# Last LayerNorm 1 block set ahead of its neighbour's block sums, with three pairs' first products in front of it in place of two

## The chip, the cores and the metric

The kernel runs on one core of a Trainium2 chip. The metric is the device time of one execution in microseconds. Before the change it was 1742.12 us, the median of three runs that lie between 1740.56 and 1743.21 us.

## The reference, cut to what matters

One decoder layer for 1024 tokens and a model width of 1024. The part around the change is the end of the mixer and the start of the MLP:

```
y = concat(SSD heads, FoX heads) @ W_out
x = LayerNorm(alpha * x + (1 + gate1) * y)            # LayerNorm 1
h = x * (1 + scale2) + shift2
x = LayerNorm(alpha * x + (1 + gate2) * (relu(h W1)^2 W2))
```

All matrices are float32. The kernel multiplies each float32 product as three matmuls of rounded parts: high times high, high times low and low times high.

## The kernel before, in words

**LayerNorm 1.** The loop at L847 goes over eight blocks of 128 tokens. For each block TensorE multiplies the second half of the mixer by W_out into two PSUM banks (`out_mm`, L853). VectorE scales the result by the RMS factor and the gate (L856) and calls `norm` (L757). `norm` adds the residual (L763), gathers mean and variance (L764, L765), adds epsilon (L766), has GpSimd raise the variance to the power -0.5 (L767, the "pow"), and scales the block. For the last block the scaling is cut in two: L769 makes a bias, L770 scales the first 512 columns on VectorE, L771 the other 512 on ScalarE. For the other blocks one VectorE instruction does it (L773).

**The block sums.** The first MLP product h W1 is computed by a Strassen-like scheme with seven products on 2 x 2 blocks in place of eight. The operands on the side of h are blocks of h (`hb_hl` 1, 2, 3) and sums of them (5, 6, 4, 7). `to_h2` (L801) makes them for one token block: eight transposes on TensorE into two PSUM tiles (L809), eight activations on ScalarE that apply scale2 and shift2 and write the tiles `h2_t` (L816; two buffers, of the tag `o_half`), the split of the lower blocks into high and low part (L823), and for token blocks 4 to 7 four differences (L827 to L830, which the profile shows at the helper's line L791). These four run on GpSimd, but for blocks 6 and 7 on VectorE. `to_h2` of a block is called one block late: block 6's behind block 7's `norm`, block 7's at L1020, behind the first products.

**The pairs.** Sixteen pairs of column blocks of W1 follow (`Pair`, L933). A pair does the products 1, 2, 5, 6, 4, 7, 3. `w1_ops` (L886) loads its weights and gives the operands one by one: those of products 1 and 2 are plain quarters, while for product 5 and the rest four GpSimd sums of 128 x 512 come first (L923 to L926). Each operand is split by ScalarE (high, L81) and VectorE (low, L85) into a `w_op` tile. Products 1 and 2 need only `hb_hl` 1 and 2, which are made from token blocks 0 to 3. So pairs 0 and 1 do products 1 and 2 (48 matmuls of 128 x 512) ahead of the last `to_h2`. Then four `h_split` calls (L1024 to L1027) split the sums of all eight blocks into `h2_s` tiles, of which product 5 needs those of L1024 first.

**PSUM.** There are eight banks: one of the tag `mm`, two of `t`, one of `o`, and two tiles of two banks each of the tag `S`. Pairs 0 and 1 hold mm, o and t, t for products 1 and 2, and take one S tile each later. From pair 2 on a pair holds either mm, o, t, t or both S tiles. The transposes of `to_h2` and the small RMS sums (L621) use S tiles as well.

**The order of the work.** The program is written in one order, and when it is built a planner puts every engine's instructions in a fixed queue, by the times of its own simulation and with preference for what is written earlier. `after(ins)` (L70) makes everything that the block issues on the engine of `ins` come behind `ins` in that engine's queue. On the chip each queue then runs strictly in order. All DMAs are issued from SP's queue.

Of the kernel before, what the change touches and what calls it, by code (L numbers as in the profile page):

```python
# [11 lines left out]
AF = mybir.ActivationFunctionType  # L12
ALU = mybir.AluOpType
# [3 lines left out]
P = 128  # L17
# [3 lines left out]
TB = T // P  # L21
# [11 lines left out]
def layer_kernel(ctx, tc, x, xT, cols, rows3, w_ada, b_ada, w_in, w_dtf, w_out, ln_rows, w1, w2, out):  # L33
    nc = tc.nc
# [15 lines left out]
    def T4(tag, name, dt=F32, shape=(P, 1024)):  # L50
        return sb.tile(list(shape), dt, name=name, tag=tag, bufs=SLOTS[tag])
# [6 lines left out]
    def PT(tag, name, shape=(P, 512), dt=F32):  # L58
        return ps.tile(list(shape), dt, name=name, tag=tag, bufs=PB[tag])
# [9 lines left out]
    @contextmanager  # L69
    def after(ins):  # L70

        with tc.issue_after(ins.ins):
            yield

    def split(raw, hi, lo, hi_eng="pool", scale=None, lo_eng="dve"):

        if scale is None:
            if hi_eng == "pool":
                nc.gpsimd.tensor_scalar(hi, raw, 1.0, 1.0, op0=ALU.mult, op1=ALU.mult)  # L79
            elif hi_eng == "act":  # L80
                nc.scalar.copy(hi, raw)  # L81
            else:
                nc.vector.tensor_copy(hi, raw)
            eng = nc.vector if lo_eng == "dve" else nc.gpsimd
            eng.tensor_tensor(lo, raw, hi.bitcast(F32), op=ALU.subtract)  # L85
        else:
            nc.scalar.activation(hi, raw, AF.Copy, scale=scale)
            nc.vector.scalar_tensor_tensor(lo, raw, scale, hi.bitcast(F32), op0=ALU.mult, op1=ALU.subtract)
# [17 lines left out]
    mhalf = cst.tile([P, 8], F32, name="mhalf")  # L106
# [31 lines left out]
    marks = {}  # L138
# [27 lines left out]
    NP = NF // 2  # L166
# [65 lines left out]
    def proj(w, half, M=P, o=None, tag="mm", ks=range(KT)):  # L232
        if o is None:
            o = PT(tag, "mm_ps")
        ts = slice(half * 512, half * 512 + 512)
        for k in ks:
            whi, wlo = wk_(w, k)
            mm(o[:M], whi, hT[k][0][:, ts], k == 0, False)
            mm(o[:M], whi, hT[k][1][:, ts], False, False)
            mm(o[:M], wlo, hT[k][0][:, ts], False, k == KT - 1)  # L240
        return o
# [18 lines left out]
    for half in range(2):  # L260
        o = proj([dtf_t[:, :, 0:4, :], dtf_t[:, :, 4:8, :]], half, 32, tag=("mm", "o")[half])
        nc.vector.tensor_copy(dtf_raw[:32, half * 512:half * 512 + 512], o[:32])
    tp = PT("t", "t_ps", (P, 8, 32))
# [7 lines left out]
    u, s_, s2, q_ = (wk[:, i, :] for i in range(4))  # L271
# [485 lines left out]
    def norm(u, o, last):  # L757

        st = sm.tile([P, 2, 6], F32, name="bn", tag="bn", bufs=2)
        mv = sm.tile([P, 4], F32, name="mv", tag="mv", bufs=2)  # L760
        for i in range(2):
            ds = slice(i * 512, i * 512 + 512)
            nc.vector.tensor_tensor(u[:, ds], o[i], u[:, ds], op=ALU.add)  # L763
            nc.vector.bn_stats(st[:, i, :], u[:, ds])  # L764
        nc.vector.bn_aggr(mv[:, 0:2], st)  # L765
        nc.vector.tensor_scalar(mv[:, 2:3], mv[:, 1:2], LN_EPS, None, op0=ALU.add)  # L766
        nc.gpsimd.tensor_tensor(mv[:, 3:4], mv[:, 2:3], mhalf[:, 0:1], op=ALU.pow)  # L767
        if last:
            nc.vector.scalar_tensor_tensor(mv[:, 2:3], mv[:, 0:1], -1.0, mv[:, 3:4], op0=ALU.mult, op1=ALU.mult)  # L769
            nc.vector.tensor_scalar(u[:, :512], u[:, :512], mv[:, 0:1], mv[:, 3:4], op0=ALU.subtract, op1=ALU.mult)  # L770
            nc.scalar.activation(u[:, 512:], u[:, 512:], AF.Identity, bias=mv[:, 2:3], scale=mv[:, 3:4])  # L771
        else:
            nc.vector.tensor_scalar(u, u, mv[:, 0:1], mv[:, 3:4], op0=ALU.subtract, op1=ALU.mult)  # L773

# [15 lines left out]
    def sub(eng, o, a, b):  # L790
        eng.tensor_tensor(o, a, b, op=ALU.subtract)  # L791
# [9 lines left out]
    def to_h2(tb, u):  # L801
        js = slice(tb % 4 * P, (tb % 4 + 1) * P)
        eng = nc.vector if tb >= TB - 2 else nc.gpsimd
        hts = []
        for hb in range(2):
            tp = PT("S", "t_ps")
            for b in range(4):
                k = hb * 4 + b
                nc.tensor.transpose(tp[:, b * P:(b + 1) * P], u[:, k * P:(k + 1) * P], identf)  # L809
            if tb < 4:  # L810
                ht = hf[hb][:, :, js]
            else:
                ht = sm.tile([P, 4, P], F32, name="h2_t", tag="o_half", bufs=2)
            for b in range(4):
                k = hb * 4 + b
                nc.scalar.activation(ht[:, b, :], tp[:, b * P:(b + 1) * P], AF.Identity, bias=b2t[:, k:k + 1],  # L816
                                     scale=g2t[:, k:k + 1])
            hts.append(ht)
            o = (1, 2)[hb] if tb < 4 else (None, 3)[hb]
            if o:  # L820
                for i in range(2):
                    t = hb_hl[o][i]
                    split(ht[:, 2 * i:2 * i + 2, :], t[:, :, 0, js], t[:, :, 1, js], "act")  # L823
        if tb >= 4:
            b12, b22 = hts
            t1, t4 = hf[0][:, :, js], hf[1][:, :, js]
            sub(eng, t1, b12, t1)  # L827
            sub(eng, t3f[:, :, js], b22, b12)
            sub(eng, t2f[:, :, js], b22, t1)
            sub(eng, t4, t4, t2f[:, :, js])  # L830
        store(x2d[tb], u)

    def u_pre(tb):

        u = T4("misc", "u1")
        load(u, u0d[tb])
        xt = T4("raw", "x_t")
        load(xt, x[tb * P:(tb + 1) * P, :])
        nc.gpsimd.tensor_tensor(u, u, g1row, op=ALU.mult)
        nc.vector.scalar_tensor_tensor(u, xt, ALPHA, u, op0=ALU.mult, op1=ALU.add)  # L840
        return u
# [3 lines left out]
    before = None  # L845
    u = u_pre(0)
    for tb in range(TB):  # L847
        ynext = y_block(1, tb + 1, "cum") if tb + 1 < TB else None
        os_ = []
        for half in range(2):  # L850
            ds = slice(half * 512, half * 512 + 512)
            o = PT(("mm", "o", "t", "t")[(2 * tb + half) % 4], "mm_ps")
            out_mm(o, y, wo, half, range(KT))  # L853
            if half == 1 and ynext is not None:
                y_rms(ynext)
            nc.vector.scalar_tensor_tensor(o, o, y[1], g1row[:, ds], op0=ALU.mult, op1=ALU.mult)  # L856
            os_.append(o)
        norm(u, os_, last=tb == TB - 1)
        if before is not None:
            to_h2(*before)  # L860
        before = (tb, u)
        y = ynext
        if tb + 1 < TB:
            u = u_pre(tb + 1)
# [68 lines left out]
    class Pair:  # L933
        def __init__(self, n):
            self.n = n
            self.w = w1_ops(n)
            self.ready = []
            if n < 2:
                zv = None
                self.bank = {b: PT(t, "f_ps") for b, t in zip("XY", (("mm", "o"), ("t", "t"))[n])}  # L940
            elif n % 2 == (n < 7):
                xy, zv = PT("S", "f_ps", (P, 1024)), PT("S", "f_ps", (P, 1024))
                self.bank = {"X": xy[:, :512], "Y": xy[:, 512:], "Z": zv[:, :512], "V": zv[:, 512:]}
            else:
                self.bank = {b: PT(t, "f_ps") for b, t in zip("XYZV", ("mm", "o", "t", "t"))}
            self.e = T4("ex", "f_e", shape=(P, 4, 512))
            self.c = HX("a_c")
            self.s = None
# [63 lines left out]
            store(ad[5:7, :, at, :].rearrange("o p c -> p o c"), t)  # L1012

    ORDER = (1, 2, 5, 6, 4, 7, 3)
    first = [Pair(0), Pair(1)]
    for p in first:
        p.run(ORDER[:2])
    for p in first:
        p.ready.append(next(p.w))
    to_h2(*before)  # L1020
    for p in first:
        zv = PT("S", "f_ps", (P, 1024))
        p.bank.update(Z=zv[:, :512], V=zv[:, 512:])
    h_split(5, lambda k: hf[0][:, k, :], ["qk"] * 4)  # L1024
    h_split(6, lambda k: t2f[:, k, :], ["qk"] * 4)
    h_split(4, lambda k: hf[1][:, k, :], ["v", "v", "w", "w"])
    h_split(7, lambda k: t3f[:, k, :], ["pt"] * 4)  # L1027
    for p in first:
        p.run(ORDER[2:])
    for n in range(2, NP):  # L1030
        Pair(n).run(ORDER if n < NP - 1 else (5, 4, 1, 6, 7, 2, 3))


# [64 lines left out]
    X = [xb[j // 2][:, j % 2 * 512:j % 2 * 512 + 512] for j in range(4)]  # L1098
    product(1, X, True, False)
    take(11, X)  # L1100
    Y = [PT(t, "y_ps") for t in ("mm", "o", "t", "t")]
# [10 lines left out]
    for tb in range(TB):  # L1112
        x2 = T4("misc", "x2")
        load(x2, x2d[tb])
        for h in range(2):
            ds = slice(h * 512, h * 512 + 512)
            o = RES[(11, 12, 21, 22)[tb // 4 * 2 + h]][:, tb % 4, :]
# [4 lines left out]
    Y = [PT(t, "y_ps") for t in ("mm", "o", "t", "t")]  # L1122
# [42 lines left out]
    for tb in range(TB):  # L1165
# [4 lines left out]
        for half in range(2):  # L1170
            ds = slice(half * 512, half * 512 + 512)
# [4 lines left out]
        mv = norm2(us, oh)  # L1176
        if not last:
            nc.vector.scalar_tensor_tensor(mv[:, 2:3], mv[:, 0:1], -1.0, mv[:, 3:4], op0=ALU.mult, op1=ALU.mult)
        for h, u in enumerate(us):
            ds = slice(h * 512, h * 512 + 512)  # L1180
# [66 lines left out]
```

## Time and profile before

| | before |
|---|---|
| median of three runs | 1742.12 us |
| range of the runs | 1740.56 to 1743.21 us |
| profiled execution | 1744.44 us, its span 1742.7 us |
| TensorE busy | 1654.0 us, 95% of the span |
| VectorE busy | 1229.9 us, 71% |
| GpSimd busy | 821.6 us, 47% |
| ScalarE busy | 747.2 us, 43% |
| mean granted TensorE clock | 0.98 |

TensorE is busy nearly all the time, so time is to be found where it stops. The lists of instructions in order of time show for each piece its start, its length, its engine and line, and in brackets how long the engine had been idle and what ended that. The pieces of one engine can overlap a little, since the next starts while the one before drains. PEclk is the granted clock of TensorE as a share of full speed.

### The profile page before, as it was taken

What the parts mean: (1) busy time and instruction counts of PE and PEld (TensorE: products, weight loads), DVE (VectorE), ACT (ScalarE), POOL (GpSimd) and SP (SyncE); (2) the same over time, 40 slices, a digit from 0 to 9 for tenths busy, and PEclk for the clock granted to TensorE, in tenths of its full rate; (3) what the DMA queues carried; (4) which work ended last, traced back from release to release, by engine and by line L of the source; (5) the groups of instructions that cost most, each with busy time, mean ns of one, the idle gap of its engine ahead of it and who ended that gap; (6) DMA issues with size and microseconds to landing.
All of it is one profiled execution on the core that took longest, in us unless ns stands there. A gap on an engine that the chain in (4) does not pass through costs nothing.

```text
span 1742.7 us, 22932 instructions
## 1 busy us (share of the span) xinstructions
PE 1654.0 (95%) x8316; PEld 1368.7 (79%) x8316; DVE 1229.9 (71%) x1898; ACT 747.2 (43%) x1321; POOL 821.6 (47%) x670
## 2 busy tenths in 40 slices
PE   8989899899999999999899999799999999999996
PEld 6777787788877878888778887688888878888885
DVE  7755777686777777676665379986767855646668
ACT  3458355414444444444565334633332334343322
POOL 5121332256566466454442345566656624704535
PEclk9999999999999999999999999899999999999998
DMA  8134343334444534434324644043444596676512
GB/s 331 37 123 147 109 145 109 121 130 151 161 142 170 169 134 167 137 121 132 119 97 130 221 157 169 37 175 133 146 143 160 172 340 212 247 242 205 194 36 96
DMA packets 112032, 268.72 MB, mean 154 GB/s; under 512 B 10128, under 2 KB 37008, under 8 KB 111920
## 3 DMA queue, kind: packets, MB, share of 16 engines
q1 hardware_dynamic: 111920, 267.27, 44.2%
q8 instruction: 65, 1.06, 0.3%
q14 instruction: 47, 0.39, 0.1%
HBM read 194.22 MB, written 64.62 MB: 149 GB/s over the span
## 4 chain that ended last, share of the span: by engine, by line
PE 60%; DVE 15%; DMA 8%; ACT 7%; POOL 5%; issue 4%; SPq 0%; DVEq 0%; ACTq 0%; POOLq 0%
PE mm_ps L62 18%; PE f_ps L957 15%; PE s_ps L1073 9%; PE y_ps L1073 7%; PE s_ps L62 5%; PE o_ps L62 4%; DVE ada_red L134 3%; PE t_ps L546 3%; DMA w_b<-in_w_dram 2%; ACT scores L417 2%; POOL w_b L182 2%; DMA raw_ada<-in_w_ada_dram 1%; DVE w_hl L85 1%; DVE conv_a L346 1%; DVE h_hl L85 1%
## 5 line engine op out<-in xcount | busy, mean ns | idle before, releaser
L62 PE MATMUL mm_ps<-h_hl,w_hl 128*128 128x512 f32 x2016 | 504.5, 400 | 10.9 <-POOL w_hl L79 6.1
L62 PEld LDWEIGHTS mm_ps<-h_hl,w_hl 128*128 128x128 f32 x2016 | 373.5, 191 | 88.3 <-POOL w_hl L79 6.9
L85 DVE TENSOR_TENSOR w_op<-raw_w,w_op 128x512 fp32r<-128x512 f32 (+1 forms) x149 | 186.9, 1260 | 23.2 <-ACT w_op L81 22.6
L957 PE MATMUL f_ps<-h_s,w_op 128*128 128x512 f32 x768 | 183.8, 394 | 6.4 <-ACT h_s L81 3.3
L957 PEld LDWEIGHTS f_ps<-h_s,w_op 128*128 128x128 f32 x768 | 146.0, 190 | 38.4 <-ACT h_s L81 3.7
L524 POOL TENSOR_SCALAR probs<-probs,m 128x128 f32<-128x128 f32 (+7 forms) x128 | 104.5, 822 | 127.3 <-DVE m L523 122.8
L81 ACT CAST w_op<-raw_w 128x512 fp32r<-128x512 f32 (+1 forms) x149 | 114.5, 774 | 100.2 <-PE f_ps L957 53.0
L1073 PE MATMUL s_ps<-w_op,a_op 128*128 128x512 f32 x672 | 153.7, 390 | 1.5 <-DVE a_op L85 1.1
L1073 PEld LDWEIGHTS s_ps<-w_op,a_op 128*128 128x128 f32 x672 | 125.9, 188 | 28.8 <-DVE a_op L85 1.6
L79 POOL TENSOR_SCALAR w_hl<-raw_w 128x512 fp32r<-128x512 f32 x86 | 60.5, 705 | 180.0 <-PE mm_ps L62 126.1
L85 DVE TENSOR_TENSOR a_op<-a_ld,a_op 128x1024 fp32r<-128x1024 f32 x53 | 75.5, 1427 | 98.4 <-ACT a_op L81 98.4
L132 POOL TENSOR_TENSOR raw_ada<-raw_ada,c_act 128x1024 f32<-128x1024 f32 x44 | 88.8, 2027 | 117.1 <-DMA raw_ada<-in_w_ada_dram 99.8
L522 ACT ACTIVATE probs<-probs,m 128x128 f32<-128x128 f32 (+7 forms) x128 | 99.1, 775 | 96.8 <-DVE m L521 86.5
L957 PE MATMUL f_ps<-h_hl,w_op 128*128 128x512 f32 x576 | 136.9, 389 | 0.0
L85 DVE TENSOR_TENSOR w_hl<-raw_w,w_hl 128x512 fp32r<-128x512 f32 x88 | 81.5, 929 | 68.5 <-POOL w_hl L79 68.2
L548 ACT CAST pt_hl<-t_ps 128x512 fp32r<-128x512 f32 (+1 forms) x160 | 84.8, 542 | 100.7 <-PE t_ps L546 97.3
L957 PEld LDWEIGHTS f_ps<-h_hl,w_op 128*128 128x128 f32 x576 | 108.0, 188 | 22.4
L81 ACT CAST a_op<-a_ld 128x1024 fp32r<-128x1024 f32 x53 | 55.7, 1054 | 159.7 <-PE s_ps L1073 80.7
L62 PE MATMUL o_ps<-pt_hl,v_s 128*128 128x256 f32 (+1 forms) x640 | 110.9, 300 | 8.7 <-DVE pt_hl L549 5.4
L549 DVE TENSOR_TENSOR pt_hl<-t_ps,pt_hl 128x512 fp32r<-128x512 f32 (+1 forms) x160 | 99.6, 630 | 23.1 <-ACT pt_hl L548 21.6
L519 DVE CUSTOM_DVE_ANT_0 probs<-s_ps,cumrow 128x128 f32<-128x128 f32 (+7 forms) x128 | 94.8, 750 | 28.9 <-PE s_ps L62 20.1
L1073 PE MATMUL y_ps<-w_op,a_op 128*128 128x512 f32 x504 | 114.7, 389 | 0.0
(254 smaller groups left out, 3136.1 us busy)
## 6 DMA issues: line engine op xcount, KB each, us to landing
raw_w<-in_w_dram SPq DMA_DIRECT2D x57, 512.0 KB, 4.3
a_ld<-ad SPq DMA_DIRECT2D x49, 512.0 KB, 4.4
raw_ada<-in_w_ada_dram SPq DMA_DIRECT2D x48, 512.0 KB, 3.6
raw_w<-in_w_in_dram SPq DMA_DIRECT2D x44, 512.0 KB, 3.7
w_b<-in_w_dram SPq DMA_DIRECT2D x14, 1024.0 KB, 8.0
w2t<-w_b SPq DMA_DIRECT2D x14, 1024.0 KB, 4.3
ad<-a_s SPq DMA_DIRECT2D x28, 512.0 KB, 3.4
raw_w<-w2t SPq DMA_DIRECT2D x28, 512.0 KB, 4.8
```

What stands on the lines that cost most here:

```text
L62: nc.tensor.matmul(o, l, r, start=start, stop=stop)
L79: nc.gpsimd.tensor_scalar(hi, raw, 1.0, 1.0, op0=ALU.mult, op1=ALU.mult)
L81: nc.scalar.copy(hi, raw)
L85: eng.tensor_tensor(lo, raw, hi.bitcast(F32), op=ALU.subtract)
L132: nc.gpsimd.tensor_tensor(raw, raw, c_act.unsqueeze(2).broadcast_to([P, KT, P]), op=ALU.mult)
L519: nc.vector.tensor_tensor_reduce(out=pt, in0=sp[:, :W], in1=cum[:, :W], op0=ALU.add, op1=ALU.max, scale=1.0, scalar=-3.0e38, accum_out=m[: ...
L522: nc.scalar.activation(pt, pt, AF.Exp, bias=m[:, 1:2], scale=1.0, accum_out=m[:, 2:3])
L524: nc.gpsimd.tensor_scalar(pt, pt, m[:, 3:4], 1.0, op0=ALU.mult, op1=ALU.mult)
L548: nc.scalar.copy(hl[:, 0, :n], tp[:, :n])
L549: nc.vector.tensor_tensor(hl[:, 1, :n], tp[:, :n], hl[:, 0, :n].bitcast(F32), op=ALU.subtract)
L957: nc.tensor.matmul(o, l, r, start=first and k == 0 and m == 0, stop=last and k == 3 and m == 2, skip_group_check=True)
L1073: nc.tensor.matmul(banks[j], ahl[a_][:, n, js], whl[w_][:, n, :], start=first and d == 0 and n == 0 and m == 0, stop=last and d == ND - 1 ...
```

## The change

For the last block the bias and the ScalarE half are gone, and VectorE scales both halves; the pow and the second half are kept as marks. Block 6's `to_h2` is put behind the second half: this binds what it issues on VectorE. The transposes of a block share one PSUM tile of two banks. Three pairs do their products 1 and 2 ahead of the last `to_h2`; the third operand of pairs 0 and 1, with its GpSimd sums, is put behind the pow and behind the scaling. Pair 2 holds one S tile for its first products, pair 1 takes o and t for its other two banks, and the later pairs take both S tiles when their number is even.

```diff
@@ norm
-        nc.gpsimd.tensor_tensor(mv[:, 3:4], mv[:, 2:3], mhalf[:, 0:1], op=ALU.pow)
+        marks["pow"] = nc.gpsimd.tensor_tensor(mv[:, 3:4], mv[:, 2:3], mhalf[:, 0:1], op=ALU.pow)
         if last:
-            nc.vector.scalar_tensor_tensor(mv[:, 2:3], mv[:, 0:1], -1.0, mv[:, 3:4], op0=ALU.mult, op1=ALU.mult)
-            nc.vector.tensor_scalar(u[:, :512], u[:, :512], mv[:, 0:1], mv[:, 3:4], op0=ALU.subtract, op1=ALU.mult)
-            nc.scalar.activation(u[:, 512:], u[:, 512:], AF.Identity, bias=mv[:, 2:3], scale=mv[:, 3:4])
+            for i in range(2):
+                ds = slice(i * 512, i * 512 + 512)
+                marks["ln"] = nc.vector.tensor_scalar(u[:, ds], u[:, ds], mv[:, 0:1], mv[:, 3:4], op0=ALU.subtract,
+                                                      op1=ALU.mult)
@@ to_h2
+        tps = PT("S", "t_ps", (P, 1024))
         for hb in range(2):
-            tp = PT("S", "t_ps")
+            tp = tps[:, hb * 512:hb * 512 + 512]
@@ loop over blocks
-        if before is not None:
+        if before is not None and tb == TB - 1:
+
+            with after(marks["ln"]):
+                to_h2(*before)
+        elif before is not None:
             to_h2(*before)
@@ Pair.__init__
-            elif n % 2 == (n < 7):
+            elif n == 2:
+                xy = PT("S", "f_ps", (P, 1024))
+                self.bank = {"X": xy[:, :512], "Y": xy[:, 512:]}
+            elif n % 2 == 0:
@@ first pairs
-    first = [Pair(0), Pair(1)]
+    first = [Pair(n) for n in range(3)]
     for p in first:
         p.run(ORDER[:2])
-    for p in first:
-        p.ready.append(next(p.w))
+    with after(marks["ln"]), after(marks["pow"]):
+        for p in first[:2]:
+            p.ready.append(next(p.w))
     to_h2(*before)
-    for p in first:
-        zv = PT("S", "f_ps", (P, 1024))
-        p.bank.update(Z=zv[:, :512], V=zv[:, 512:])
...
     for p in first:
+        if p.n == 1:
+            p.bank.update(Z=PT("o", "f_ps"), V=PT("t", "f_ps"))
+        else:
+            zv = PT("S", "f_ps", (P, 1024))
+            p.bank.update(Z=zv[:, :512], V=zv[:, 512:])
         p.run(ORDER[2:])
-    for n in range(2, NP):
+    for n in range(3, NP):
```

## Rows read from the trace of the kernel before

**Rows 1.** The busy time of each engine over the whole span, in us, as a share of the span, and the number of instructions.
```profile
PE 1654.0 (95%) x8316; PEld 1368.7 (79%) x8316; DVE 1229.9 (71%) x1898; ACT 747.2 (43%) x1321; POOL 821.6 (47%) x670
```

**Rows 2.** Busy time by stretch around the end of LayerNorm 1. The columns are the stretch, its length, the busy time and the number of instructions of each engine, the granted TensorE clock, the DMA share and GB/s. The last row is a stretch of the pairs well behind the change.
```profile
1100.00:1110.00 10.00, 6.03 (x27) 4.67 (x25) 9.96 (x14) 1.55 (x3) 8.69 (x7) 1.00 0.00 0
1110.00:1120.00 10.00, 4.19 (x13) 2.92 (x14) 8.85 (x13) 10.00 (x24) 2.99 (x2) 0.52 0.14 55
1120.00:1130.00 10.00, 10.00 (x37) 8.01 (x37) 10.00 (x18) 7.56 (x16) 0.64 (x1) 0.79 0.00 0
...
1140.00:1160.00 20.00, 20.00 (x90) 16.57 (x89) 17.20 (x17) 7.33 (x13) 16.74 (x11) 1.00 0.51 186
```

**Rows 3.** TensorE in order of time, from the first products of the pairs on: start, length, engine, line, tiles, count, and the idle time before with what ended it.
```profile
1094.86 11.17 PE L957 MATMUL f_ps<-h_hl,w_op 128*128 128x512 f32 x48
1110.16 1.68 PE L809 MATMUL t_ps<-identf,u 128*128 128x128 f32 x8 [4.13 <-DVE u L770]
1115.09 1.22 PE L957 MATMUL f_ps<-h_s,w_op 128*128 128x512 f32 x2 [3.25 <-ACT h_s L81]
1118.71 21.42 PE L957 MATMUL f_ps<-h_s,w_op 128*128 128x512 f32 x82 [2.40 <-DVE h_s L85]
```

**Rows 4.** The same columns as in Rows 2, for single microseconds in which the granted clock falls and rises.
```profile
1110.00:1111.00 1.00, 0.84 (x6) 0.87 (x7) 1.00 (x3) 1.00 (x3) 0.00 (x0) 0.73 0.00 0
...
1123.00:1124.00 1.00, 1.00 (x4) 0.72 (x4) 1.00 (x3) 0.82 (x3) 0.00 (x0) 0.50 0.00 0
1124.00:1125.00 1.00, 1.00 (x6) 0.82 (x5) 1.00 (x3) 0.42 (x1) 0.00 (x0) 0.95 0.00 0
```

**Rows 5.** Pieces of the chain of work that ended last: start, length, and engine, tile and line. The last is its first long piece on TensorE behind the change.
```profile
1108.42 1.15 DVE mv L769
1109.59 0.81 ACT u L771
...
1118.71 61.31 PE f_ps L957 x258
```

**Rows 6.** VectorE in order of time, with the columns of Rows 3, from block 6's scaling to the low parts of the first sums.
```profile
1091.50 1.77 DVE L773 TENSOR_SCALAR u<-u,mv 128x1024 f32<-128x1024 f32 x1 [0.67 <-POOL mv L767]
...
1094.58 2.80 DVE L85 TENSOR_TENSOR h_hl<-h_t,h_hl 128x256 fp32r<-128x256 f32 x2
...
1097.91 1.17 DVE L85 TENSOR_TENSOR w_op<-raw_w,w_op 128x512 fp32r<-128x512 f32 x1
1099.00 0.75 DVE L856 SCALAR_TENSOR_TENSOR mm_ps<-mm_ps,r_rms,g1row 128x512 f32<-128x512 f32 x1
1099.67 1.12 DVE L85 TENSOR_TENSOR w_op<-raw_w,w_op 128x512 fp32r<-128x512 f32 x1
1100.70 0.68 DVE L763 TENSOR_TENSOR u<-mm_ps,u 128x512 f32<-128x512 f32 x1
1101.42 0.69 DVE L764 BATCH_NORM_STATS2 bn<-u 128x6 f32<-128x512 f32 x1
1102.03 1.70 DVE L791 TENSOR_TENSOR h_f<-h_t,h_f 128x512 f32<-128x512 f32 x1
...
1103.77 1.65 DVE L791 TENSOR_TENSOR h_t<-h_t 128x512 f32<-128x512 f32 x1
1105.34 0.14 DVE L766 TENSOR_SCALAR mv<-mv 128x1 f32<-128x1 f32 x1
1105.40 0.68 DVE L791 TENSOR_TENSOR h_t<-h_t,h_f 128x512 f32<-128x512 f32 x1
1106.00 0.75 DVE L85 TENSOR_TENSOR h_hl<-h_t,h_hl 128x256 fp32r<-128x256 f32 x2
1106.67 1.75 DVE L791 TENSOR_TENSOR h_f<-h_f,h_t 128x512 f32<-128x512 f32 x1
1108.34 1.21 DVE L769 SCALAR_TENSOR_TENSOR mv<-mv 128x1 f32<-128x1 f32 x1
1109.48 0.54 DVE L770 TENSOR_SCALAR u<-u,mv 128x512 f32<-128x512 f32 x1
...
1112.87 0.69 DVE L791 TENSOR_TENSOR h_f<-h_t,h_f 128x512 f32<-128x512 f32 x1 [0.45 <-ACT h_t L816]
1114.26 0.69 DVE L791 TENSOR_TENSOR h_t<-h_t 128x512 f32<-128x512 f32 x1 [0.70 <-ACT h_t L816]
...
1115.47 1.50 DVE L85 TENSOR_TENSOR h_hl<-h_t,h_hl 128x256 fp32r<-128x256 f32 x1
```

**Rows 7.** GpSimd in order of time, with the same columns: a sum of a pair's weights, the last block's pow, the last sums of pair 1, and the next sum.
```profile
1091.43 1.29 POOL L791 TENSOR_TENSOR w_s<-raw_w 128x512 f32<-128x512 f32 x1
...
1105.56 0.93 POOL L767 TENSOR_TENSOR mv<-mv,mhalf 128x1 f32<-128x1 f32 x1 [0.69 <-ACT w_op L81]
1106.46 3.08 POOL L791 TENSOR_TENSOR raw_w<-raw_w 128x512 f32<-128x512 f32 x2
1115.03 1.66 POOL L791 TENSOR_TENSOR w_s<-raw_w 128x512 f32<-128x512 f32 x1 [5.50 <-DVE h_t L791]
```

**Rows 8.** SP's queue in order of time: the last early load of weights, and the stores of blocks 6 and 7.
```profile
1089.11 0.33 SPq L65 DMA_DIRECT2D raw_w<-in_w_dram  x1
1093.30 17.45 SPq L65 DMA_DIRECT2D x2d<-u  x2
```

**Rows 9.** Who TensorE waited for between 1000 and 1125 us: in total, how often, the longest.
```profile
PE t_ps L809 <- DVE r_rms L624: 2.3, 2, 1.2
```

## The prediction

> **What bounds the kernel now.** I read the engine shares first: TensorE is busy 95% of the span, VectorE 71% [rows 1]. So time can only be won where TensorE stops or runs slowly, and the table of stretches shows such a place at the seam between LayerNorm 1 and the pairs: 6.03 us busy out of ten from 1100 us, 4.19 from 1110, and a granted clock of 0.52 and 0.79 in the two stretches from 1110 and from 1120 [rows 2]. TensorE's own order of time says what it lacks there. After 48 early matmuls it stops 4.13 us until block 7's scaling (L770) lets the transposes start, then 3.25 us for the high and 2.40 us for the low parts of the first sums [rows 3]. That is 9.8 us, and with the clock falling from full (2.4 GHz) to half (1.2 GHz) at about 1110.7 us and rising at about 1124, it works at half rate from 1118.7 to 1124, which costs another 2.7 us [rows 3, 4].
>
> The chain of waits says who is late: it leaves VectorE only for ScalarE pieces near 1110 and joins TensorE at 1118.71 [rows 5]. VectorE was busy 9.96 us out of ten from 1100 [rows 2]. In its queue, block 6's four differences (1.70, 1.65, 0.68, 1.75 us) and two low splits (0.75 together) stand ahead of or between the last steps of block 7's norm, and L769 takes 1.21 us for a 128 x 1 result [rows 6]. The reader should see two prices for the same kind of instruction: a 128 x 512 difference is 0.68 us where GpSimd is idle (1105.40) and 1.7 us where GpSimd runs its own sums. The instructions that read PSUM (0.69 and 0.75) or do statistics (0.69) keep their price [rows 6, 7].
>
> **The change, part by part.** The profiled execution took 1744.44 us with a span of 1742.7; the median of the runs is 1742.12, 2.3 lower. I work out a difference on this trace and take it off the median. About 0.2% (3.5 us) is what a measurement can tell from no change.
>
> *Pair 2's first two products.* 24 matmuls move into the hole. Well behind the seam 90 take 20 us, 0.222 each [rows 2], so later work shrinks by 5.3 us. At the early rate, 48 in 11.17 us or 0.233 each [rows 3], 72 end at 1094.86 + 16.8 = 1111.6. This is the gain of the whole change: as TensorE has the transposes behind these products, it can't profit from anything earlier.
>
> *The transposes.* They start at about 1111.6 in place of 1110.16 [rows 3], 1.4 us later, if block 7 is scaled by then. Were they put between the pairs, the delay would be 0.
>
> *Block 7's norm.* From 1094.58 to the end of L770 at 1110.02 VectorE spends 15.4 us. Block 6's work, 6.5 us, and L769, 1.2 us, leave it. The second half adds 0.54, and the wait for the pow, filled by block 6 before, is now bare: 0.67 as it was for block 6 [rows 6]. Pair 2's first split takes the place of one of pair 0's, which moves behind the norm. That gives 1103.5. GpSimd's weight sums, which began at 1091.43, now start behind the pow, so the stretch in front of it is quieter: of the two low splits at 2.80 one at 0.4 and one at 1.5 remain, and two weight splits fall from 1.17 and 1.12 to 0.68 [rows 6, 7], 1.8 us less. Block 7 is scaled by 1101.7, ten microseconds ahead of TensorE.
>
> *VectorE until block 7's first difference* (1112.87 before, after 0.45 us of idle time). It does the same work in another order plus two splits for pair 2: one quiet (0.68), one beside GpSimd (1.12), together +1.8. The second half against L769 is -0.7, the bare wait +0.7, the quiet stretch -1.8. GpSimd's eight sums now all run from the pow on, beside block 6's work. I price it that the one difference that ran alone goes from 0.68 to 1.75 and one low split from 0.4 to 1.5 [rows 6], +2.2. Sum +2.2, less the two idle waits of 0.45 and 0.70 that it fills: +1.0. Bounds: both splits quiet and no clash added, -1.5; every clash, see the second rival.
>
> *What sets the resumption.* VectorE asks for +1.0, TensorE's transposes for +1.4; the later counts. So the sums and with them the work of 1118.71 come 1.4 us later, with 5.3 us less to do: a gain of **3.9 us**. Between no delay and the VectorE bound of the second rival it is 5.3 to 1.3.
>
> *The clock.* TensorE now works at full speed until 1111.6 and then waits once for the sums, still some 5 to 7 us with little in between. I take the half-rate stretch as it was, worth nothing; the bound is the 2.7 us that it costs now.
>
> *Edits taken at nothing.* The moved sums of pairs 0 and 1 are eight of 1.3 to 1.6 us [rows 7], about 12 us from the pow at 1101: pair 0's second is done by 1104, pair 1's second by 1110, ahead of the resumption. If GpSimd were late, each would cost TensorE its own 1.5 us. GpSimd's next sum waited 5.50 us for block 7's differences before [rows 7] and still does. ScalarE gives up L771 (0.81 us on the chain, rows 5), and its part is priced above. SP's queue holds block 7's store until L771's half is done, 17.45 us in one piece [rows 8]; it comes free earlier, and pair 2's last early load was issued at 1089.11 ahead of it, so nothing is late. Sharing one PSUM tile for the eight transposes takes away two waits for the RMS sums, 2.3 us together [rows 9]; at that time VectorE is what TensorE's results wait for, so I give it 0, up to 2.3. The later pairs' banks: pair 1's o and t come free with its first products' results, and even pairs still alternate with odd ones. Should one be late, TensorE waits for one PSUM read of 0.7 us.
>
> **The rivals.** *The clock stays up.* One wait in place of two may not bring it down. For it: until 1111.6 TensorE has no hole left. Against it: the 4.13 us stop was followed by the fall [rows 3, 4], and the remaining wait is as long. Then 2.7 us more are won: 3.9 + 2.7 = 6.6, 1735.5 us.
>
> *VectorE and GpSimd block each other all the way.* From 1101.7 nine two-input instructions (block 6's six, three weight splits) meet eight GpSimd sums. At 1.75 us for eight and 0.68 for the last, VectorE reaches block 7's first difference at 1116.4, not at 1112.42 when it came free before: 4.0 us later, a gain of 1.3, 1740.8 us. For it: three of block 6's four differences had this price [rows 6]. Against it: the fourth and the two low splits at 1106.00 hardly had, with GpSimd busy for half the time. The Trainium skill, page "SBUF — State Buffer", section "Who interferes with whom", says that a VectorE instruction with two SBUF inputs and a GpSimd instruction that reads SBUF exclude each other for the whole instruction; by that rule it would be this case. The trace agrees as far as it goes: 1.7 against 0.68.
>
> *Pair 2's second operand comes late (slower).* Its place is VectorE's queue. Its `w_op` tile needs a buffer that pair 0's first product frees at 1094.86 + 2.8 = 1097.7. If the planner therefore sets its low split behind block 6's six instructions, it ends at 1101.7 + 7 x 1.75 = 1114.0. TensorE has run out after 60 matmuls at 1108.8 and stands 5.1 us, with block 7's transposes queued behind the 12 that are left: 1116.8 against 1110.16, 6.6 us late. A stop of that length is followed by the half clock, as the 4.13 us one was, and the 12 cost 2.8 us more. Sum 5.3 - 6.6 - 2.8 = -4.1: 1746.2 us. It decides from a split that ends after 1108.8 and loses from about 1112.7 on. For it: the norm alone is pinned ahead of block 6, not the split. Against it: written earlier, it is preferred, and ScalarE had little to do before 1105.
>
> *The change does not do what it says*, since the scaling ends no earlier: TensorE is then covered until 1111.6 all the same and block 6's 6.5 us fall behind 1110. That is the second rival's time, and part of its chance.
>
> **How the numbers follow.** The forecast 60%: 1742.12 - 3.9 = 1738.2 us; with its own bounds (gain 1.3 to 5.3, and up to 1.5 more where upstream waits give something back) it lies above 3.5 us in 41 of the 60. Clock stays up 10%, faster. Mutual blocking 16%: 14 same, 2 slower. Late operand 14%: 10 slower, 4 same where the split is less late. Faster 0.51, same 0.37, slower 0.12. The range reaches from 1733.5 (clock up, and 2 us of the bounds) to 1743.5, past the second rival and short of the full price of the third.
>
> **What would show it.** In the changed profile: 72 early matmuls without a gap from about 1095 to 1111.6; block 7's scaling near 1102 with block 6's differences behind it; transposes right behind the 72 with no wait for L770's successor; the next matmul on sums at about 1120, a wait of some 7 us in all, and the half clock to about 1125; no new wait for PSUM banks in the pairs. It is wrong if TensorE stops after 48 or 60 matmuls, if the resumption lies beyond 1122, or if the clock holds at 1.00.

## The result, and the profile after

The change made the kernel slower: 1755.31 us (median of six runs, 1754.55 to 1757.95) against 1741.36 us for the kernel before in the same session (six runs, 1740.03 to 1743.21), a ratio of 1.0082 with an interval of 1.0069 to 1.0095. The profiled execution took 1756.47 us with a span of 1754.7, 12.0 us more than before. TensorE's busy time hardly moved (1652.4 us against 1654.0 in [rows 1]), so the time was lost in stops.

TensorE of the kernel after in order of time, with the columns of [rows 3]. It stands against those rows:

```profile
1087.39 6.88 PE L966 MATMUL f_ps<-h_hl,w_op 128*128 128x512 f32 x29
1094.11 0.60 PE L811 MATMUL t_ps<-identf,u 128*128 128x128 f32 x4
1094.46 7.33 PE L966 MATMUL f_ps<-h_hl,w_op 128*128 128x512 f32 x31
1101.63 0.60 PE L811 MATMUL t_ps<-identf,u 128*128 128x128 f32 x4
1107.20 1.11 PE L811 MATMUL t_ps<-identf,u 128*128 128x128 f32 x4 [4.97 <-ACT h_t L818]
1111.12 0.80 PE L966 MATMUL f_ps<-h_s,w_op 128*128 128x512 f32 x1 [2.81 <-ACT h_s L81]
1112.28 4.28 PE L966 MATMUL f_ps<-h_s,w_op 128*128 128x512 f32 x11 [0.36 <-DVE h_s L85]
1129.98 17.17 PE L966 MATMUL f_ps<-h_s,w_op 128*128 128x512 f32 x62 [13.42 <-ACT f_e L979]
```

Sixty matmuls (29 + 31) stand ahead of block 7's transposes, not 72. The second half of these transposes waits 4.97 us, until ScalarE has read the first half, which lies in the same tile. Then product 5 of pair 0 runs (1 + 11 matmuls), and TensorE stops for **13.42 us**: product 6 adds to the bank that ScalarE's copy of product 1 (L979) has to read first. What ScalarE does until then, in order of time:

```profile
1104.08 1.66 ACT L81 CAST w_op<-raw_w 128x512 fp32r<-128x512 f32 x3 [3.86 <-POOL raw_w L789]
1105.65 1.50 ACT L818 ACTIVATE h_t<-t_ps,b2t,g2t 128x128 f32<-128x128 f32 x4
...
1117.32 2.17 ACT L81 CAST h_s<-h_f 128x512 fp32r<-128x512 f32 x4
1119.39 0.61 ACT L81 CAST w_op<-w_s 128x512 fp32r<-128x512 f32 x1
1128.30 0.62 ACT L81 CAST w_op<-raw_w 128x512 fp32r<-128x512 f32 x1 [8.30 <-POOL raw_w L792]
1128.83 0.61 ACT L81 CAST w_op<-w_s 128x512 fp32r<-128x512 f32 x1
1129.35 0.58 ACT L979 COPY f_e<-f_ps 128x512 f32<-128x512 f32 x1
```

The copy needs nothing that is late. Two casts stand ahead of it in the queue. The first, of `raw_w`, is pair 2's operand of product 3, which comes from the last of GpSimd's four sums for pair 2. No product needs this operand for a long time yet. GpSimd's queue shows why the sums are late (these rows stand against [rows 7]), and VectorE's what runs meanwhile:

```profile
1111.10 13.15 POOL L792 TENSOR_TENSOR w_s<-raw_w 128x512 f32<-128x512 f32 x1 [3.97 <-DVE h_t L792]
1124.33 1.26 POOL L789 TENSOR_TENSOR raw_w<-raw_w 128x512 f32<-128x512 f32 x1
1125.67 2.60 POOL L792 TENSOR_TENSOR raw_w<-raw_w 128x512 f32<-128x512 f32 x2
```

```profile
1094.90 2.94 DVE L771 TENSOR_SCALAR u<-u,mv 128x512 f32<-128x512 f32 x2 [0.45 <-POOL mv L767]
...
1109.74 0.68 DVE L792 TENSOR_TENSOR h_f<-h_t,h_f 128x512 f32<-128x512 f32 x1
1110.34 0.68 DVE L792 TENSOR_TENSOR h_t<-h_t 128x512 f32<-128x512 f32 x1
...
1115.23 4.89 DVE L85 TENSOR_TENSOR h_s<-h_t,h_s 128x512 fp32r<-128x512 f32 x8
1120.04 2.48 DVE L85 TENSOR_TENSOR h_s<-h_f,h_s 128x512 fp32r<-128x512 f32 x4
1122.45 0.68 DVE L85 TENSOR_TENSOR w_op<-w_s,w_op 128x512 fp32r<-128x512 f32 x1
1128.95 0.69 DVE L85 TENSOR_TENSOR w_op<-raw_w,w_op 128x512 fp32r<-128x512 f32 x1 [5.82 <-ACT w_op L81]
```

One sum of the kind that took 1.66 us before [rows 7] takes 13.15 us. It lasts through an unbroken row of VectorE instructions with two SBUF inputs, and ends 1.1 us after the last of them (1122.45 + 0.68 = 1123.13, against 1111.10 + 13.15 = 1124.25).

The first two lines of ScalarE show the same pattern on a smaller scale. Block 7's first transposes are done at 1102.23, but ScalarE reads them only from 1105.65 on, behind three casts of weights, for the first of which it waited 3.86 us on a GpSimd sum that the change had moved. That makes TensorE's 4.97 us so long. It costs nothing that can be seen, since VectorE has no pause before block 7's first difference at 1109.74.

Of the waits of TensorE from 980 us to the end, with the columns of [rows 9], those on r_rms shown there are gone, and those on VectorE's low parts of the weights (L85) are 3.6 us (0.8 before):

```profile
PE f_ps L966 <- DVE w_op L85: 3.6, 4, 1.4
```

Busy time by stretch, with the columns of [rows 2]:

```profile
1100.00:1110.00 10.00, 3.34 (x16) 2.34 (x15) 10.00 (x10) 4.79 (x12) 6.97 (x5) 0.76 0.00 1
1110.00:1120.00 10.00, 5.08 (x12) 3.37 (x12) 10.00 (x18) 9.55 (x19) 8.90 (x1) 0.67 0.00 0
1120.00:1130.00 10.00, 0.02 (x1) 0.02 (x1) 4.18 (x8) 1.70 (x5) 8.04 (x4) 0.50 0.00 0
1130.00:1140.00 10.00, 10.00 (x32) 8.05 (x33) 4.82 (x8) 3.25 (x6) 0.00 (x0) 0.70 0.00 0
```

**The account of the profiled executions.** The first early matmul starts 7.5 us sooner (1087.39 against 1094.86). Of this, 3.7 us were there already at the last step of L659, in work that the change does not touch; 3.8 us come from the rest of the LayerNorm 1 stage. From that matmul to the first one of the second stage it is 339.2 us against 321.3, 17.9 us more: the stop 13.4; waits on `w_op` 3.6 - 0.8 = 2.8; half clock after the stops, 9.2 us of work at it against 5.4, half of the difference, 1.9; the sums 24.9 us behind the first early matmul against 23.9, 1.0; less 12 x 0.222 = 2.7 for what moved ahead. That is 16.4; 1.5 us of the 17.9 stay unassigned. In the second stage 1.6 us more go with a dip of the clock (0.66 from 1429 to 1434 us). The sum, 17.9 + 1.6 - 7.5, is the 12.0 of the spans.

### The profile page after: what moved, and what is told of

It reads as the page before. It is cut to its first block, busy times and chain, and to the rows that moved or that the text cites. A ratio compares the mean times of both kernels' runs of the same rounds, so it can differ in the third digit from the quotient of the medians.

```text
span 1754.7 us, 22925 instructions
## 1 busy us (share of the span) xinstructions
PE 1652.4 (94%) x8316; PEld 1364.6 (78%) x8316; DVE 1234.9 (70%) x1898; ACT 746.5 (43%) x1320; POOL 829.7 (47%) x670
## 5 line engine op out<-in xcount | busy, mean ns | idle before, releaser
L85 DVE TENSOR_TENSOR w_op<-raw_w,w_op 128x512 fp32r<-128x512 f32 (+1 forms) x149 | 193.2, 1303 | 34.7 <-ACT w_op L81 34.2
L966 PE MATMUL f_ps<-h_s,w_op 128*128 128x512 f32 x768 | 185.6, 397 | 17.4 <-ACT f_e L979 13.4
L85 DVE TENSOR_TENSOR a_op<-a_ld,a_op 128x1024 fp32r<-128x1024 f32 x53 | 76.8, 1450 | 99.1 <-ACT a_op L81 99.0
L85 DVE TENSOR_TENSOR w_hl<-raw_w,w_hl 128x512 fp32r<-128x512 f32 x88 | 79.5, 906 | 66.1 <-POOL w_hl L79 65.9
L62 PE MATMUL o_ps<-pt_hl,v_s 128*128 128x256 f32 (+1 forms) x640 | 106.5, 290 | 8.5 <-DVE pt_hl L549 4.6
```

Source lines behind the costliest of these rows:

```text
L62: nc.tensor.matmul(o, l, r, start=start, stop=stop)
L966: nc.tensor.matmul(o, l, r, start=first and k == 0 and m == 0, stop=last and k == 3 and m == 2, skip_group_check=True)
```

## The experiments

Before's median lies between 1741.4 and 1742.5 us in all sessions. "Stop" is TensorE's wait for pair 0's copies, "sum" the first GpSimd sum of pair 2; both are read from the one profiled execution of each kernel.

| kernel | transposes' PSUM | block 7 first | pairs ahead | pair 2's cast | median us | sum us | stop us |
|---|---|---|---|---|---|---|---|
| before | two tiles | no | 2 | | 1742.5 | 1.66 | none |
| shared transposes only | one tile | no | 2 | | 1737.84 | 13.19 | 0.57 |
| LayerNorm first only | two tiles | yes | 2 | | 1743.98 | 13.18 | 0.96 |
| both of these | one tile | yes | 2 | | 1740.85 | 13.17 | 1.78 |
| three pairs, old norm, cast moved | one tile | no | 3 | behind | 1744.67 | 13.78 | 4.05 |
| three pairs, old norm | one tile | no | 3 | ahead | 1753.12 | 13.15 | 12.64 |
| after, cast moved | one tile | yes | 3 | behind | 1745.97 | 13.78 | 3.71 |
| after | one tile | yes | 3 | ahead | 1755.31 | 13.15 | 13.42 |

### The cast behind the copies

```diff
-                    nc.scalar.copy(p1, bank["X"])
+                    marks["p1", self.n] = nc.scalar.copy(p1, bank["X"])
...
-        p.run(ORDER[2:])
+        if p.n == 2:
+            with after(marks["p1", 1]):
+                p.run(ORDER[2:])
+        else:
+            p.run(ORDER[2:])
```

> The changed kernel, with one instruction of ScalarE's queue moved: pair 2's first cast that needs GpSimd's sums (the operand of product 3) comes behind the copies of pairs 0 and 1 out of PSUM in place of two places ahead of pair 0's. Theory A (a queue made the stop: the cast waits for GpSimd's sums of pair 2, which VectorE's unbroken run of splits holds up, and pair 0's copy stands behind the cast): the stop of 13.4 us falls to about 4, what is left being the splits and casts that the copy has to wait for in any case; about 9.5 us faster than the changed kernel, some 1745 us, while GpSimd's sum still takes over 10 us. Theory B (the PSUM plan: with three pairs nothing else is left for TensorE): the stop stays above 10 us, 1753 to 1757 us. Theory C (VectorE itself is slowed by GpSimd): no change either, and the first sums' splits no shorter.

Measured: 1745.97 us, ratio to before 1.0025 (1.0013 to 1.0037). In the queues two instructions have changed places: this cast, four places further back in ScalarE's (behind the other cast and three copies), and its low part, two places further back in VectorE's. ScalarE and GpSimd of this run:

```profile
1118.54 1.13 ACT L81 CAST w_op<-w_s 128x512 fp32r<-128x512 f32 x2
1119.57 0.57 ACT L979 COPY f_e<-f_ps 128x512 f32<-128x512 f32 x1
...
1128.16 0.62 ACT L81 CAST w_op<-raw_w 128x512 fp32r<-128x512 f32 x1 [7.06 <-POOL raw_w L792]
```

```profile
1110.24 13.78 POOL L792 TENSOR_TENSOR w_s<-raw_w 128x512 f32<-128x512 f32 x1 [3.97 <-DVE h_t L792]
```

The sum is as slow as before the edit; the cast waits for it as long; but the copy no longer does. The stop falls from 13.42 to 3.71 us, 9.7 us, and the median by 9.3, as theory A expected. So two thirds of the loss are the place of one cast in ScalarE's queue, together with a GpSimd sum that is held.

### LayerNorm first alone, and three pairs without it

Of the change, the first kernel keeps only the new order of norm and the third operands of pairs 0 and 1 behind it, with two pairs. The second is the kernel after with the old norm, scaled by VectorE and ScalarE behind block 6's sums; these lines of its edit leave the pinning out:

```diff
-    with after(marks["ln"]), after(marks["pow"]):
-        for p in first[:2]:
-            p.ready.append(next(p.w))
+    for p in first[:2]:
+        p.ready.append(next(p.w))
```

> The kernel before with only the reordering of the norm: block 7's scaling on VectorE alone and ahead of block 6's sums, the third operands of pairs 0 and 1 behind it; two early pairs, transposes in two PSUM tiles. By the prediction's sum the stop of 4.13 us before the transposes goes, and VectorE's work up to block 7's first difference is about the same: 0 to 3 us faster than the kernel before, 1738 to 1741.5 us. Theory A: no stop for a copy, since no pair 2 is in the queues yet. Rival (the reordering by itself starves GpSimd): a new stop of 5 us or more here too, 1746 us or more.

> The changed kernel with the norm's old order: three early pairs and the new PSUM plan, but block 7's scaling in two halves on VectorE and ScalarE behind block 6's sums, and nothing pinned. ScalarE's queue again has pair 2's cast ahead of pair 0's copy, and GpSimd's sums of pair 2 behind block 7's differences. Theory A: a stop of about 10 to 14 us as in the changed kernel, 1752 to 1757 us. Rival (the reordered norm made the stop): no stop above 5 us, 1737 to 1742 us.

Measured: 1743.98 us, ratio 1.0012 (1.0000 to 1.0025), and 1753.12 us, 1.0064 (1.0042 to 1.0086). LayerNorm first gains nothing and misses its forecast of 0 to 3 us. The transposes no longer wait for block 7's scaling, and the stop comes one step later, as this run of TensorE shows:

```profile
1091.94 11.14 PE L962 MATMUL f_ps<-h_hl,w_op 128*128 128x512 f32 x48
1102.93 1.03 PE L810 MATMUL t_ps<-identf,u 128*128 128x128 f32 x8
1114.71 1.22 PE L962 MATMUL f_ps<-h_s,w_op 128*128 128x512 f32 x2 [10.75 <-ACT h_s L81]
```

Before it was 4.13 + 3.25 + 2.40 = 9.78 us [rows 3], here 10.75 + 0.27. VectorE has to get through the same differences first. Most of the loss is there without LayerNorm first (ratio 1.0064, against 1.0082 for the whole change), with a stop of 12.64 us.

### VectorE's row broken

The kernel after; the low parts of the sums 6, 4 and 7 are left out and filled with zeros, so that each of VectorE's twelve splits with two inputs becomes two zero fills, which are set behind the splits of L1024.

```diff
-            split(src(k), t[:, 0, :], t[:, 1, :], "act")
...
+                nc.scalar.copy(t[:, 0, :], src(k))
+                with after(marks["h5"]):
+                    for _ in range(2):
+                        nc.vector.memset(t[:, 1, :].bitcast(F32), 0.0)
```

> The changed kernel with VectorE's twelve low splits of the sums for products 6, 4 and 7 replaced by two fills with zero each (the low parts of these sums are left out), which read nothing. If VectorE's instructions with two inputs hold up GpSimd, pair 2's first sum takes under 4 us in place of 13.15; if that sum is slow for a reason of its own, it stays above 8 us. The planner puts pair 0's copy ahead of the cast here, so the total is not comparable; by theory A it lies near 1743 us.

Measured, one run: 1745.92 us. GpSimd's sum:

```profile
1113.18 4.69 POOL L792 TENSOR_TENSOR w_s<-raw_w 128x512 f32<-128x512 f32 x1 [3.97 <-DVE h_t L792]
```

4.69 us in place of 13.15: it ends 1.2 us after VectorE's last two-input instruction ahead of the fills (1115.43 + 1.28 = 1116.71), while the fills go on. So the row of two-input instructions is what holds it, though the figure is above the 4 us expected. The total says less, since the planner put the copy ahead of the cast here too.

### The shared transpose tile alone, and with each of the other parts

```diff
+        tps = PT("S", "t_ps", (P, 1024))
         for hb in range(2):
-            tp = PT("S", "t_ps")
+            tp = tps[:, hb * 512:hb * 512 + 512]
```

> The kernel before with one part of the change alone: the two transpose tiles of a block are the halves of one tile of two PSUM banks. If the 3.8 us that the LayerNorm 1 stage became shorter after the change come from this part (TensorE no longer waits there for the r_rms tiles), this kernel is 2 to 4 us faster than before: 1738 to 1740 us, with the first W_f product some 3.8 us sooner after the last load-side step of ScalarE than before (94.9 against 98.7 us). Rival: the second half of a block's transposes must then wait for the reading of the first half (4.97 us for block 7 after the change), and eats the gain: 1742 to 1745 us.

> The kernel before with two parts of the change, the shared transpose tile and block 7's LayerNorm first, two pairs ahead as before. The shared tile alone gave 1737.84 us, LayerNorm first alone gave nothing (1743.98). Theory: VectorE's work sets when the W_f sums go on, so LayerNorm first gives nothing here either: 1736 to 1740 us. Rival: LayerNorm first costs time by itself, because its steps stand ahead of work that the sums need: 1741 to 1745 us.

> The kernel after without block 7's LayerNorm first, and with ScalarE's cast put behind the copies: third pair and shared transpose tile alone. With the shared tile alone (1737.84), the shared tile and LayerNorm first, and the whole change with the cast moved (1745.97) it makes a square. Theory: the third pair costs the 6 to 8 us between 1738 and 1746 whichever way LayerNorm stands, since VectorE, which sets when the sums go on, has pair 2's splits ahead of them: 1742 to 1746 us, with a stop behind pair 0's copy of 3 to 5 us. Rival: the third pair is harmless once the cast is moved, and LayerNorm first is what costs: 1736 to 1740 us.

Measured: 1737.84 us, ratio 0.9975 (0.9964 to 0.9985); 1740.85, 0.9993 (0.9979 to 1.0008), between the two ranges that were expected; 1744.67, 1.0013 (1.0000 to 1.0026). This part alone has **the lowest median of the study** and is faster than before and after; the kernel before with one-bank tiles (1738.36, below) can't be told from it. TensorE with the shared tile alone:

```profile
1101.37 0.60 PE L810 MATMUL t_ps<-identf,u 128*128 128x128 f32 x4
1105.40 0.65 PE L810 MATMUL t_ps<-identf,u 128*128 128x128 f32 x4 [3.43 <-ACT h_t L817]
1109.98 8.85 PE L958 MATMUL f_ps<-h_s,w_op 128*128 128x512 f32 x24 [3.93 <-ACT h_s L81]
1119.40 13.89 PE L958 MATMUL f_ps<-h_s,w_op 128*128 128x512 f32 x60 [0.57 <-ACT f_e L971]
```

The RMS waits of 2.3 us [rows 9] are gone, and the seam costs 3.43 + 3.93 = 7.4 us in place of 9.8: 4.7 us together, as much as the median fell. (The two profiled executions differ by 8.0 us, so this is a sum of the main waits and no full account.) GpSimd's sum is held in this run too (13.19 us) and costs nothing, since no cast that needs it stands ahead of a copy. The square then reads, downwards: shared tile -4.7, LayerNorm first +3.0 on top, the third pair with the cast moved +5.1, the cast's place +9.3. Each step is uncertain by some 3 us, since each ratio is by some 2. In the other order the third pair is +6.8 and LayerNorm first +1.3. So it is shown that the third pair costs time and that the two cost 8.1 us together, but not that LayerNorm first costs any. With the third pair, the stop behind pair 0's copy is 4.05 us against 0.57 and the `w_op` waits 3.6 against 0.8. That is 6.3 us more, against 2.7 for the twelve matmuls that moved; the medians differ by 6.8 us and the profiled executions by 3.5, so the size of this step is not settled.

### Tiles of one bank

From the last LayerNorm 1 stage on, four PSUM tiles of one bank take the place of two tiles of two banks (a transpose tile is one bank again). The first kernel has this with the change and the cast moved, the second on the kernel before, the third with the change and the cast left ahead.

```diff
-                xy = PT("S", "f_ps", (P, 1024))
-                self.bank = {"X": xy[:, :512], "Y": xy[:, 512:]}
+                self.bank = {b: PT("S", "f_ps") for b in "XY"}
```

> The kernel after with ScalarE's cast put behind the copies of pairs 0 and 1, and with four PSUM tiles of one bank each in place of the tiles of two banks from the last LayerNorm 1 stage on (the two transpose tiles of a block are separate again). Theory: only 12 of pair 2's 24 first matmuls moved, and the second half of block 7's transposes waited 5.0 us, because a tile of two banks is freed and waited for as one. Then 72 matmuls stand ahead of block 7's transposes, no second half waits, and of the 1746 us of the kernel with the cast alone moved some 3 to 8 us go: 1738 to 1743 us. Rival: VectorE sets when the W_f sums go on in any case (122.5 us after the marker in before and with the early LayerNorm alone), so that more early matmuls only lengthen the early part and shorten the late one: 12 x 0.226 = 2.7 us at most, 1743 to 1746 us.

> The kernel before with the four PSUM tiles of one bank alone (nothing of the change). It is the measure for the run with one-bank tiles on top of the change: if the tile form alone is worth nothing, 1741 to 1743 us; if the tiles of two banks delayed the pairs of the kernel before as well, or the second stage, 1737 to 1741 us.

> The kernel after with the four PSUM tiles of one bank, and ScalarE's cast left where the change has it, ahead of pair 0's copy. If the cast in ScalarE's queue is the main cause and the tile form a small one, TensorE still stops for about 10 to 13 us behind pair 0's copy: 1747 to 1753 us. Rival: if the tile form is the main cause, the stop is mostly covered by the products that the free banks let run: 1738 to 1745 us.

Measured: 1740.72 us, ratio 0.9994 (0.9981 to 1.0007); 1738.36, 0.9980 (0.9966 to 0.9994); 1744.23, 1.0012 (1.0001 to 1.0022). TensorE of the first:

```profile
1093.63 14.31 PE L968 MATMUL f_ps<-h_hl,w_op 128*128 128x512 f32 x62
1109.18 2.60 PE L968 MATMUL f_ps<-h_hl,w_op 128*128 128x512 f32 x10 [1.24 <-DVE w_op L87]
1111.61 1.04 PE L815 MATMUL t_ps<-identf,u 128*128 128x128 f32 x8
1116.09 0.56 PE L968 MATMUL f_ps<-h_s,w_op 128*128 128x512 f32 x1 [3.44 <-ACT h_s L83]
1119.69 3.34 PE L968 MATMUL f_ps<-h_s,w_op 128*128 128x512 f32 x6 [3.04 <-DVE h_s L87]
```

Now all 72 matmuls run ahead of the transposes and no half of these waits for the other: both were the tile of two banks, which is freed and waited for as one. Yet the kernel is not faster than the one with one-bank tiles alone, which was itself 4.1 us faster than the kernel before and had no RMS waits either. Its 72 matmuls last 18.2 us (the forecast had 16.8), until 1111.8, and only then do block 7's transposes start; the way from there to the first sums is bare again, 3.44 + 3.04 us and more.

The third kernel has the cast ahead of the copy and no stop for it, against its expectation of 10 to 13 us, because GpSimd's sum was not held. Its GpSimd and ScalarE:

```profile
1114.36 1.65 POOL L797 TENSOR_TENSOR w_s<-raw_w 128x512 f32<-128x512 f32 x1 [5.74 <-DVE h_t L797]
```

```profile
1123.97 1.17 ACT L83 CAST w_op<-raw_w 128x512 fp32r<-128x512 f32 x2
1125.31 0.58 ACT L981 COPY f_e<-f_ps 128x512 f32<-128x512 f32 x1 [0.17 <-DVE h_s L87]
```

Its time lies in the rival's range, but not by the rival's mechanism: no long wait for the copy was covered by other products, there was none.

So the big stop needs both: the sum held, and the cast ahead. Where GpSimd gets in, VectorE pays: in this run two of its splits took 3.44 us in place of 1.28.

### Pair 2's first products behind block 7's transposes

The kernels with one-bank tiles and with the shared tile, both with the cast moved:

```diff
-    for p in first:
+    for p in first[:2]:
         p.run(ORDER[:2])
...
     to_h2(*before)
+    first[2].run(ORDER[:2])
```

> The kernel with one-bank tiles and the cast moved (1740.72 us), but with pair 2's first products put behind block 7's transposes in the program, so that they run while ScalarE and VectorE work on block 7: 48 matmuls, 8 transposes, 24 matmuls. In the run with 72 ahead of the transposes TensorE stopped 3.4 + 3.0 + 0.6 us behind them. Theory: the change fills no idle time because it lengthens what stands ahead of block 7's transposes; put behind them, 24 matmuls (5.4 us) fill most of these stops: 1735 to 1738 us. Rival: VectorE sets when the sums go on, it has pair 2's splits to do in either order, and the time stays within 2 us: 1739 to 1742.5 us.

> The kernel after with the cast moved (1745.97 us), tiles of two banks as in the change, and pair 2's first products behind block 7's transposes in the program: 12 matmuls then stand between the two halves of these transposes, where TensorE waited 4.97 us, in place of 60 matmuls ahead of them. Theory as for the run with one-bank tiles: 2 to 5 us come back, 1741 to 1744 us. Rival: the wait for the reading of the first half was no part of what set the sums, and nothing changes: 1745 to 1747 us.

Measured: 1739.20 us, ratio 0.9983 (0.9970 to 0.9996), and 1751.17, 1.0057 (1.0036 to 1.0077). TensorE of the first:

```profile
1106.28 1.03 PE L815 MATMUL t_ps<-identf,u 128*128 128x128 f32 x8
1107.07 1.17 PE L968 MATMUL f_ps<-h_hl,w_op 128*128 128x512 f32 x4
1113.83 6.41 PE L968 MATMUL f_ps<-h_hl,w_op 128*128 128x512 f32 x20 [5.60 <-DVE w_op L87]
1120.08 2.88 PE L968 MATMUL f_ps<-h_s,w_op 128*128 128x512 f32 x12
```

The products are where the hole is, and the hole moves in front of them: pair 2's low splits wait in VectorE's queue. The first result lies in the rival's range and can't be told from 1740.72, nor from one-bank tiles alone. The second went against both expectations, 5 us slower: 4.74 us for pair 2's cast, 2.79 for its split, both ahead of block 7's second transposes, then 6.95 behind pair 0's copy.

## Why the prediction was wrong, step by step

The forecast was a gain of 3.9 us; the change lost 14.0.

*Edits taken at nothing: the step that failed most.* The prediction saw that GpSimd's next sum waits for block 7's differences and "still does", and stopped there. Behind that sum are queued three more, behind these a ScalarE cast, and behind the cast the copy that frees pair 0's bank. The step named what the sum waits for, not who stands behind it. It also took the sum's length as given, though the second rival has VectorE and GpSimd block each other, only with VectorE as the slowed one. Here GpSimd was slowed: 13.15 us for 1.66. That the place of the cast behind the held sum is worth 9.3 us of the 14.0 is shown by the run with the cast moved, and without LayerNorm first it is 8.5 (1753.12 - 1744.67).

*The later pairs' banks, at most "one PSUM read of 0.7 us", failed.* Before, product 5 of pairs 0 and 1, 24 matmuls, could run before pair 0's copy was needed. After, pair 1's product 5 uses bank o, which holds pair 0's product 2 until VectorE has added that copy to it, so 12 are left. Even with the cast moved the stop is 3.71 us, against none [rows 3].

*The 24 matmuls of pair 2 failed.* Twelve moved, 2.7 us and not 5.3: X and Y are halves of one tile, and product 2 waits for the copy that reads X. With one-bank tiles 24 moved, and nothing was won by it. So the sentence that this is "the gain of the whole change" was wrong in kind. What ends the seam is VectorE's way from block 7's transposes to the first sums. Matmuls ahead of the transposes do not shorten that way, which with all 72 of them ahead still showed waits of 3.44 + 3.04 us (3.25 + 2.40 before); and matmuls behind them need splits from VectorE.

*The shared transpose tile, "0, up to 2.3", was mis-sized*: alone it lowered the median by 4.7 us, by the RMS waits and by a shorter seam. In the whole change this gain is hidden under the losses.

*Right:* block 7 was scaled before TensorE needed it (at 1097.84, its transposes at 1101.63). Counted from the first early matmul that was later than forecast, 10.5 us against 6.8, since TensorE started 7.5 us sooner in this trace. VectorE sets the resumption, at 24.9 us behind the first early matmul. The half clock came, but twice, once around each stop. Two of the prediction's own signs of being wrong came too: TensorE stopped after 60 matmuls, and there was a new wait for a PSUM bank.

*The rivals.* The third, pair 2's second operand late, had the right sign and is what two later kernels showed (5.60 us and 4.74 + 2.79), but not the kernel after, where its split is done at 1094.5 and product 2 waits for a bank. The point from which it loses, "about 1112.7", leaves out the 2.8 us of half clock that the rival itself charges; with them it is about 1109.9. The second priced VectorE's slowing at 4.0 us; here VectorE's first difference of block 7 comes 0.6 us later, counted from the last step of L659.

## What to carry to other kernels

When a step is moved ahead, follow its later instructions into every in-order queue and ask what is queued behind each of them: a cast that nobody needs yet can hold a copy that everybody needs. A change of several parts is to be run part by part; here one part of it was worth 4.7 us and the rest cost almost four times as much. Filling a stop with other work pays only if that work does not come from the engine that makes the stop.

## What the runs showed of the hardware

GpSimd's first 128 x 512 sum of pair 2 took 13.15 to 14.98 us in eight of the profiled kernels and 1.65 to 1.68 us in five, besides 4.69 with VectorE's row broken. Held sums end 1.1 to 1.2 us after the last of VectorE's row of instructions with two SBUF inputs, a little less than an undisturbed sum takes (1.26 to 1.3), so the sum seems to begin only there. In six of the eight the next VectorE instruction is a sum with one input in PSUM (`a_c<-f_ps,f_e`); it kept its 0.68 us and did not hold GpSimd any longer. Where the sum was not held, VectorE's splits of 128 x 512 beside it took about 1.75 us for 0.68. The Trainium skill, page "SBUF — State Buffer", section "Who interferes with whom", has an exclusive lock between the two, held for the whole instruction, with the order of issue deciding who blocks. The traces agree in that one side can be kept out entirely; they add that a back-to-back row of VectorE instructions can keep GpSimd out to its end and not for one instruction.

One thing separates the two outcomes in all fourteen traces. The sum is released by VectorE's second difference of block 7 (`h_t<-h_t`). In the five kernels where GpSimd got in, VectorE had paused before that difference, for 0.08 to 0.99 us (0.70 in the kernel before [rows 6]); in the nine others it had not. The shortest pause is that of one-bank tiles with the cast ahead (1112.82 + 0.69 = 1113.51, then 1113.58):

```profile
1112.82 0.69 DVE L797 TENSOR_TENSOR h_f<-h_t,h_f 128x512 f32<-128x512 f32 x1
1113.58 0.69 DVE L797 TENSOR_TENSOR h_t<-h_t 128x512 f32<-128x512 f32 x1
```

In the kernel after the two overlap (1109.74 + 0.68 = 1110.42, against 1110.34). No run changed the pause alone, so that it decides is not shown.
